# One product pair, the joining of product banks and four loads, rearranged in a decoder block on one core

## The chip, the cores and the metric

The kernel runs on one core of one Trainium2 chip. The metric is the device time of one execution in microseconds (us). Before the change, three runs took 1681.38, 1682.75 and 1682.48 us; the median is 1682.48 us. One further execution was profiled.

The core's engines work side by side and wait for each other by semaphores: TensorE (PE, matrix multiply; PEld is its weight load), VectorE (DVE), ScalarE (ACT), GpSimd (POOL) and SyncE (SP, which here only issues DMAs).

## The reference

One layer on 256 tokens of width 2048, in float32, cut to what matters:

```python
def token_mixers(x, ...):
    proj = x @ w_in                       # (256, 2048) x (2048, 13336)
    ...                                   # gated linear attention and forgetting attention
    merged = sigmoid(ma) * y_gla + sigmoid(mb) * y_fox
    return merged @ w_out

def conv_gated_mlp(x, w_gate, w_up, conv_w, conv_b, w_down):
    g = causal_dwconv(x @ w_gate, conv_w, conv_b)
    h = jax.nn.gelu(g) * (x @ w_up)       # (256, 5632)
    return h @ w_down

x = layer_norm(ALPHA * x + mix, ln1_g, ln1_b)
x = layer_norm(ALPHA * x + ffn, ln2_g, ln2_b)
x = x + sigmoid(x @ w_ple_gate) * (p @ w_ple_proj)
```

## The kernel before

**Split matmuls.** Every float32 operand is split in two: `hi`, a rounded copy made by ACT (`copy`, L106), and `lo = raw - hi`, made by DVE (L170). A product is three matmuls, hi by hi, hi by lo and lo by hi. Weights stream from memory in *units* of 1 MB (two tiles of 128 x 1024). `unit()` (L178) hands out the next unit and first calls `prep()` so that units up to two ahead are loaded and split: two DMAs on SP's queue into a ring of four `raw` tiles (L165, L166), then `hi` and `lo` into six buffers each. SP's instructions keep program order, set by hand (L108). On the other engines a planner orders the instructions before the run: it follows a clock of its own, takes what is ready there, higher priority first, and gives out buffers as it goes. The chip then executes each engine's list in that order.

**Half products.** `x_half` (L323) computes 256 tokens by 1024 columns: four PSUM banks (two token tiles t by two column blocks c), and a loop over units i, where a unit covers the pair of 128-row blocks 2i and 2i+1 of the contraction. A plain unit is 24 matmuls of 512 columns (`x_mm`, L267). After unit i it runs `mid[i]()` if there is one; that is where residual tiles and norm rows are loaded. Units kept for the *tail* are done bank by bank, so that banks finish one after the other, token tile 0 first; each is then evacuated by `evac`.

**Seven products.** Pairs listed in `ws` (`DNP`: pairs 2, 4, ..., 18 of each half of the down projection `dn`) are computed by `seven` (L283): the pair is a 2 x 2 block product, done with seven block products in place of eight, 21 matmuls. Three of them accumulate straight into the `dn` banks, four into product banks m0 to m3 (two from the pool of six `mm` banks, two from the pool of two `mx` banks) that live from the first such pair to the last. It needs sums of activation blocks, kept in DRAM (`hsd`, loaded by POOL's queue, L1095, L1096), and sums of weight blocks, made by `prep_seven` (L124: splits L135, four subtractions L140 to L143) and `split_seven` (L146: two further splits L153). A seven-product unit takes three buffers of 8 KB from the pool `big` (15 buffers): `raw` and two `ts`. hT, the MLP's activations, holds ten of them throughout `dn`; the two residual tiles `z2` and the norm rows come from the same pool.

**Joining.** After the last listed pair, `joined` (L928) adds the four product banks into the residual tiles: one ACT copy of m0 into `ju`, then eight DVE steps (L934 puts ALPHA z + sum into a tile, L938 adds a bank). Each tile z[t][:, block] then gets its own `dn` bank by `ev` (L919; L923, or L925 where there are no seven-product pairs) and its statistics (L926).

**Order of the stages.** Projections and attention; `wo` (two halves of eight units; residual tiles z1 and the first norm's gain and bias rows loaded after unit 4 of the first half, `mid1` at L998); first LayerNorm; gate and up projections; `dn` (two halves of 22 units; z2 loaded after unit 4 of the first half, `mid2` at L1157; norm rows after unit 8 of the second, `mid2a`, and the small operands of `pp` after unit 17, `mid2b`; tail of two units in the second half); second LayerNorm (`ln_out`, L827: statistics, normalisation L840 and L843, transposes on PE L846, scale and shift L853 and L855, split L857 and L858); the gate product `pg` (L1201) and the output. `pp` (24 matmuls, L988) is emitted after dn's last unit and depends on neither dn nor the LayerNorm. The residual evacuation and the statistics have the priority `P_STAT`; weight splits and the joining have none.

Of the kernel before, what the change touches and what calls it, by code (L numbers as in the profile page):

```python
# [14 lines left out]
ALU = mybir.AluOpType  # L15
# [8 lines left out]
NF = DFF // P  # L24
# [4 lines left out]
ALPHA = 2 ** 0.25  # L29
# [4 lines left out]
P_STAT = 5000  # L34
# [9 lines left out]
S8W = 2048  # L44
DN0 = 224
DNP = tuple(range(2, 20, 2))
WH = 1152
HSTEP = 48

# [5 lines left out]
def tile_block(ctx: ExitStack, tc: tile.TileContext, wu, wfv, wpp, xT_in, x_in, pT_in, wlr,  # L55
               chan, gnorm, lng, ident_in, mask_in, cmask_in, out):
    nc = tc.nc
# [15 lines left out]
    st1 = [cst.tile([P, 4, 6], F32, name=f"st1{t}") for t in range(2)]  # L73
# [13 lines left out]
    def w_tile(tag, dt, name, u):  # L87
        if tag == "lo":
            return wide.tile([P, 1024], dt, tag=tag, name=name)
        o = 0 if u in XSTAT else HSTEP  # L90
        return wide.tile([P, WH], dt, tag=tag, name=name)[:, o:o + 1024]

# [3 lines left out]
    def t2(name):  # L96
        return sm.tile([P, 512], F32, tag="t2", bufs=6, name=name)
# [7 lines left out]
    def copy(o, i, scale=1.0):  # L105
        nc.scalar.activation(o, i, AF.Copy, bias=0.0, scale=scale)  # L106
# [307 lines left out]
    for u in range(8):  # L414
        hi, lo = fvu[u]
        for j in range(2):
            kt = 2 * u + j
            a = xT[kt // 4][:, kt % 4, :]
            for cs in ((0,), (1,), (2,)) if u == 0 else ((0, 1, 2),):
                for t in range(2):  # L420
                    ah, al = a[:, t * P:t * P + P], a[:, 256 + t * P:256 + t * P + P]
                    for i, (w, x) in enumerate(((hi[j], ah), (lo[j], ah), (hi[j], al))):
                        for c in cs:
                            o, n = fch[c]
# [189 lines left out]
    for nm, dst, sc in (("q", gq, 1.0 / 16.0), ("k", gk, 1.0)):  # L614
        for n in range(8):
# [3 lines left out]
            h, c = n // 2, n % 2  # L619
# [178 lines left out]
    mT = [s8([P, 4, 512], F32R, name=f"mT{i}") for i in range(4)]  # L798
# [25 lines left out]
    x1d = dr.tile([2, P, 2048], F32, name="x1d")  # L824
# [84 lines left out]

        return stat, norm, turn  # L910

    def residual(name, act, K, zs, stats, mid, done=None, end=None, ws=()):

        for nh in range(2):
            def zp(t, c, nh=nh):
                g = 2 * nh + c
                return zs[t][:, g * 512:g * 512 + 512]

            def ev(t, c, ps, nh=nh, zp=zp):  # L919
                zc = zp(t, c)  # L920
                with tc.high_priority(P_STAT):
                    if ws:
                        nc.vector.tensor_tensor(zc, zc, ps, ALU.add)  # L923
                    else:
                        nc.vector.scalar_tensor_tensor(zc, zc, ALPHA, ps, ALU.mult, ALU.add)  # L925
                    nc.vector.bn_stats(stats[t][:, 2 * nh + c, :], zc)  # L926

            def joined(ms, zp=zp):  # L928
                p1, p5, p7, p6 = ms
                u = t2("ju")  # L930
                copy(u, p1)

                def onto(t, c, p):
                    nc.vector.scalar_tensor_tensor(zp(t, c), zp(t, c), ALPHA, p, ALU.mult,  # L934
                                                   ALU.add)

                def plus(o, a, p):
                    nc.vector.tensor_tensor(o, a, p, ALU.add)  # L938

                onto(0, 0, p1)  # L940
                plus(u, u, p6)
                onto(0, 1, u)
                plus(u, u, p7)
                onto(1, 0, u)
                plus(u, u, p5)
                onto(1, 1, u)
                plus(zp(0, 1), zp(0, 1), p5)

            x_half(f"{name}{nh}", act, K, ev, tail=2 if nh == 1 else 0, mid=mid[nh],
                   done=done if nh == 1 else None, end=end if nh == 1 else None, ws=ws,  # L950
                   joined=joined)

    def affine(zs, gb_, after, gs=range(4)):
# [15 lines left out]
    def ple_prep(half):  # L969

        w = [s8([P, 2048], F32R, name=f"pw{half}{i}") for i in range(2)]
        pt_ = s8([P, 2, 512], F32R, name=f"pTs{half}")
        pTs = [pt_[:, k, :] for k in range(2)]
        for k in range(2):
            raw = ring.tile([P, 1024], F32, tag="raw", bufs=4, name=f"praw{half}{k}")
            nc.sync.dma_start(raw, wpp[half, :, k * 1024:k * 1024 + 1024])
            o = slice(k * 1024, k * 1024 + 1024)
            copy(w[0][:, o], raw)
            nc.vector.tensor_tensor(w[1][:, o], raw, w[0][:, o].bitcast(F32), ALU.subtract)
        pT = t2("pTr").rearrange("p (k t) -> p k t", t=S)  # L980
        nc.sync.dma_start(pT, pT_in)
        for k in range(2):
            copy(pTs[k][:, 0:256], pT[:, k, :])
            nc.vector.tensor_tensor(pTs[k][:, 256:512], pT[:, k, :],
                                    pTs[k][:, 0:256].bitcast(F32), ALU.subtract)
        return w, pTs
# [8 lines left out]
    z1 = [s8([P, 2048], name=f"z1{t}") for t in range(2)]  # L995
    gain = [None, None]

    def mid1():  # L998
        for t in range(2):
            nc.sync.dma_start(z1[t], x_in[t])  # L1000
        gain[0] = load_gain(0)

    x1T = [s8([P, 4, 512], F32R, name=f"x1T{g}") for g in range(4)]
    pq, first = [], []
# [68 lines left out]
                    turn1(G[3])  # L1073
            first.extend(ps)

    residual("wo", mT, 16, z1, st1, ({4: mid1}, {3: lambda: pq.append(ple_prep(0))}), end=end1)
    mixers.append(affine(z1, gain[0], lambda t: nc.gpsimd.dma_start(x1d[t], z1[t]),
                         [g for g in range(4) if g not in AFF_DVE]))

# [7 lines left out]
    hT = [None] * 11  # L1087
    hsd = dr.tile([len(DNP), P, 2, 512], F32, name="hsd")
    before = [None]

    def h_sums(i):
        j = DNP.index(i)

# [4 lines left out]
        return load  # L1098

    for nh in range(2):  # L1100
        for i in DNP:
            sums[DN0 + nh * (NF // 2) + i] = h_sums(i)

    def lt(shape, dt, name):
# [10 lines left out]
    for n in range(NF):  # L1115
# [17 lines left out]
        u = t1("up")  # L1133
# [4 lines left out]
        nc.vector.tensor_tensor(dst[:, 256:512], y, dst[:, 0:256].bitcast(F32), ALU.subtract)  # L1138
        if n % 2 == 1 and n // 2 in DNP:
            sf = t2("hs")  # L1140
            x_sums(before[0], y, sf)
            for i, nm in enumerate(("hsh", "hsl")):
# [4 lines left out]
                else:  # L1147
                    nc.vector.tensor_tensor(sp, sf, sh.bitcast(F32), ALU.subtract)
                nc.gpsimd.dma_start(hsd[DNP.index(n // 2), :, i, :], sp.bitcast(F32))
        before[0] = y  # L1150
# [3 lines left out]
    z2 = [s8([P, 2048], name=f"z2{t}") for t in range(2)]  # L1154
    st2 = [st20, sm.tile([P, 4, 6], F32, tag="st2", bufs=1, name="st21")]

    def mid2():  # L1157
        for t in range(2):
            nc.sync.dma_start(z2[t], x1d[t])

    def mid2a():
        gain[1] = load_gain(1)
# [5 lines left out]
    pb, pq = [], []  # L1168
# [3 lines left out]
            pb.extend(ple_proj(1, *pq[0]))  # L1172
        ln_out(z2, st2, t, x2T, c_g2, c_b2, "l2", P_LN2[t])

    residual("dn", hT, NF, z2, st2, ({4: mid2}, {8: mid2a, NF // 2 - 5: mid2b}), done2, ws=DNP)
    pp = [s8([P, 2, 1024], name=f"ppk{i}") for i in range(2)]
    for t in range(2):
        for c in range(2):
# [37 lines left out]
def _xst(w):  # L1216

    k, n = w.shape
    a = w.reshape(k // 256, 2, P, n // 1024, 1024).transpose(3, 0, 2, 1, 4)
    return a.reshape((k // 256) * (n // 1024), P, 2048)  # L1220


def _swap(a, ps):

    a = a.reshape(-1, P, 4, 512)
    for n in ps:
        a[n] = a[n][:, [0, 1, 3, 2]]
    return a.reshape(-1, P, 2048)
# [7 lines left out]
def _chan(v):  # L1236
    return v.reshape(-1, P).T


def _layout(i):  # L1240
    w_in = i["w_in"][0]
    c = lambda nm, n: w_in[:, OFF[nm]:OFF[nm] + n]
    bg, bf = _wst(i["w_branch_gla"][0]), _wst(i["w_branch_fox"][0])
    br = []
    for n in range(16):
        br.append(bg[n:n + 1])
        if n % 2 == 0:
            br.append(bf[n // 2:n // 2 + 1])
    gu = np.stack([_wst(i["w_gate"][0]), _wst(i["w_up"][0])], 1).reshape(2 * NF, P, 2048)
    wu = np.concatenate(  # L1250
        [_wst(c("fq", 1024)), _wst(c("fk", 1024)), _wst(c("gq", 1024)),
         _wst(c("gk", 1024)), _xst(c("gv", 2048)), _xst(c("gr", 2048)),
         _wst(c("ma", 2048)), _wst(c("mb", 2048))] + br
        + [_xst(i["w_out"][0]), gu, _swap(_xst(i["w_down"][0]), [h * (NF // 2) + p for h in range(2) for p in DNP]),
           _xst(i["w_ple_gate"][0])], 0)
    wfv = np.concatenate([c("fv", 1024), c("glr", 16), c("ff", 8)], 1)
    wfv = wfv.reshape(8, 2, P, NS).transpose(0, 2, 1, 3)
    x = _fold(i["x"][0])
    bfo = np.zeros((P, 1), np.float32)
    bfo[:FH, 0] = i["b_forget"][0]  # L1260
    chan = np.concatenate(
        [_chan(i["b_gla_lr"][0]), bfo, _chan(i["ln1_g"][0]), _chan(i["ln1_b"][0]),
         _chan(i["ln2_g"][0]), _chan(i["ln2_b"][0])]
        + [_chan(i["conv_w"][0][j]) for j in range(3)] + [_chan(i["conv_b"][0])], 1)
    lng = np.stack([i["ln1_g"], i["ln1_b"], i["ln2_g"], i["ln2_b"]])
    s = np.arange(P)[:, None]
    t = np.arange(P)[None, :]
    masks = [s == t]
    for lev in range(1, 8):
        L = 1 << lev  # L1270
        masks.append((s // L == t // L) & (s % L < L // 2) & (t % L >= L // 2))
    mask = np.stack([m if h == 0 else m.T for m in masks for h in range(2)], 1).astype(np.float32)
    caus = np.where(t <= s, 0.0, NEG).astype(np.float32)
    cmask = np.concatenate([caus.T, caus], 1)
    return dict(wu=wu, wfv=wfv, wpp=_xst(i["w_ple_proj"][0]), xT=x.T.reshape(16, P, S).transpose(1, 0, 2),
                x=x.reshape(2, P, D), pT=_fold(i["p"][0, 0]).T.reshape(2, P, S).transpose(1, 0, 2),
                wlr=i["w_gla_lr"][0], chan=chan, gnorm=i["gla_norm_g"], lng=lng,
                ident=np.eye(P, dtype=np.float32), mask=mask, cmask=cmask)
# [20 lines left out]
```

## Time and profile before

| | |
|---|---|
| Profiled execution, time | 1681.58 us |
| Its span (first to last instruction) | 1679.8 us |
| Median of three runs | 1682.48 us |
| Mean granted TensorE clock | 0.996 |
| Busy: DVE, ACT, POOL | 71%, 52%, 4% |
| Moved by DMA | 344.39 MB, mean 205 GB/s |
| Matmul records | 8981 |

How to read it: busy time is the union of an engine's instructions, as a share of the span. Matmuls overlap in the pipeline and their ends are modelled, so PE can look busy while it issues fewer matmuls than it could; the count of matmuls in a window tells more. In a line of an engine's order the number in square brackets is the engine's idle time before the instruction, with what ended it. In a line of the waits stand total, times and longest. Times in windows and orders count from the span's start. `L170` is line 170 of the kernel. A few matmul records can be missing from a trace.

### The profile page before, as it was taken

Reading aid. Unit: us, or ns where it says so; the run is one execution under the profiler, and the core shown is the slowest. Engines: PE = TensorE matmul, PEld = TensorE weight load, DVE = VectorE, ACT = ScalarE, POOL = GpSimd, SP = SyncE. Lnnn points to the kernel's source line nnn. Section 1 sums busy time; section 2 is a strip of 40 time slices with the busy share of each in tenths; the row PEclk is TensorE's granted clock in tenths of the full one; section 3 lists DMA queues with packets and bytes.
Section 4 is the critical chain, followed back from the end, with each engine's and each line's share of the span. In section 5 each row is a group of like instructions: output and inputs, shape, how many; then the busy total and the mean of one; then the engine's idle time right before and its main releaser. Section 6 shows DMA issues by size and latency. Waiting matters only on the chain.

```text
span 1679.8 us, 24075 instructions
## 1 busy us (share of the span) xinstructions
PE 1659.1 (99%) x8981; PEld 1435.6 (85%) x8981; DVE 1196.8 (71%) x1757; ACT 866.5 (52%) x1247; POOL 64.5 (4%) x177
## 2 busy tenths in 40 slices
PE   9999999999999999999999999999999999999898
PEld 8888888888888888888788888888888887788687
DVE  6666658768756557774677777777777778998774
ACT  5645445545555544443465555555555545455543
POOL 0100000000000000000010000000000011010000
PEclk9999999999999999999999999999999999999999
DMA  7755455555555455557646676666666666696455
GB/s 268 266 191 164 163 189 182 180 177 176 184 179 175 165 195 192 195 192 258 236 152 209 229 232 206 205 207 205 209 204 208 216 248 222 236 338 245 150 180 171
DMA packets 95748, 344.39 MB, mean 205 GB/s; under 512 B 11096, under 2 KB 12768, under 8 KB 94224
## 3 DMA queue, kind: packets, MB, share of 16 engines
q1 hardware_dynamic: 90528, 324.51, 57.7%
q0 software_dynamic: 5104, 18.36, 2.9%
q8 instruction: 70, 1.15, 0.3%
q14 instruction: 46, 0.38, 0.1%
HBM read 332.85 MB, written 9.97 MB: 204 GB/s over the span
## 4 chain that ended last, share of the span: by engine, by line
PE 94%; DVE 2%; DMA 1%; ACT 1%; issue 1%; SPq 0%; POOL 0%; ACTq 0%; DVEq 0%
PE psu L236 9%; PE psg L236 9%; PE dn L280 7%; PE psm L236 7%; PE gr L280 5%; PE gv L280 5%; PE pg L280 5%; PE psu L238 5%; PE psg L238 5%; PE wo L280 4%; PE psm L238 3%; PE psa L236 3%; PE fv L425 2%; PE dn L301 2%; PE psfq L236 2%; PE psfk L236 2%
## 5 line engine op out<-in xcount | busy, mean ns | idle before, releaser
L106 ACT ACTIVATE hi<-raw 128x1024 fp32r<-128x1024 f32 (+1 forms) x568 | 591.7, 1045 | 635.4 <-issue 220.8
L170 DVE TENSOR_TENSOR lo<-raw,hi 128x1024 fp32r<-128x1024 f32 x532 | 649.4, 1222 | 359.8 <-ACT hi L106 356.8
L236 PE MATMUL psu<-x1T,hi 128*128 128x512 f32 x688 | 236.0, 389 | 0.0
L236 PE MATMUL psg<-x1T,hi 128*128 128x512 f32 x672 | 230.5, 389 | 0.0
L238 PE MATMUL psu<-x1T,lo 128*128 128x256 f32 x688 | 190.0, 276 | 0.0
L238 PE MATMUL psg<-x1T,lo 128*128 128x256 f32 x672 | 185.5, 276 | 0.0
L236 PE MATMUL psm<-xT,hi 128*128 128x512 f32 x512 | 175.8, 391 | 0.0
L236 PEld LDWEIGHTS psu<-x1T,hi 128*128 128x128 f32 x688 | 129.1, 188 | 26.8
L236 PEld LDWEIGHTS psg<-x1T,hi 128*128 128x128 f32 x672 | 126.2, 188 | 26.3
L238 PE MATMUL psm<-xT,lo 128*128 128x256 f32 x512 | 141.5, 276 | 0.0
L238 PEld LDWEIGHTS psu<-x1T,lo 128*128 128x128 f32 x688 | 129.2, 188 | 0.0
L238 PEld LDWEIGHTS psg<-x1T,lo 128*128 128x128 f32 x672 | 126.1, 188 | 0.0
L280 PE MATMUL dn<-hi,hT 128*128 128x512 f32 x416 | 118.9, 389 | 0.0
L236 PEld LDWEIGHTS psm<-xT,hi 128*128 128x128 f32 x512 | 96.2, 188 | 19.8
L238 PEld LDWEIGHTS psm<-xT,lo 128*128 128x128 f32 x512 | 96.2, 188 | 0.1
L280 PEld LDWEIGHTS dn<-hi,hT 128*128 128x128 f32 x416 | 78.0, 188 | 16.3
L236 PE MATMUL psa<-oT,hi 128*128 128x512 f32 x256 | 87.8, 389 | 0.0
L280 PE MATMUL wo<-hi,mT 128*128 128x512 f32 x256 | 71.9, 396 | 3.1 <-DVE z L925 3.0
L280 PE MATMUL gv<-hi,xT 128*128 128x512 f32 x256 | 72.3, 394 | 0.0
L280 PE MATMUL gr<-hi,xT 128*128 128x512 f32 x256 | 72.1, 394 | 0.0
L238 PE MATMUL psa<-oT,lo 128*128 128x256 f32 x256 | 70.7, 276 | 0.0
L280 PE MATMUL pg<-hi,x2T 128*128 128x512 f32 (+1 forms) x256 | 69.7, 383 | 0.0
(300 smaller groups left out, 2836.4 us busy)
## 6 DMA issues: line engine op xcount, KB each, us to landing
raw<-in_wu_dram SPq DMA_DIRECT2D x568, 512.0 KB, 4.6
fvraw<-in_wfv_dram SPq DMA_DIRECT2D x14, 524.0 KB, 7.9
hi<-hsd POOLq DMA_DIRECT2D x18, 256.0 KB, 4.8
lo<-hsd POOLq DMA_DIRECT2D x18, 256.0 KB, 5.4
lnb<-in_lng_dram SPq DMA_DIRECT2D x4, 1024.0 KB, 11.7
hsd<-hsh POOLq DMA_DIRECT2D x9, 256.0 KB, 5.6
hsd<-hsl POOLq DMA_DIRECT2D x9, 256.0 KB, 5.4
z<-in_x_dram SPq DMA_DIRECT2D x2, 1024.0 KB, 10.8
```

The costliest lines, as they stand in the source:

```text
L106: nc.scalar.activation(o, i, AF.Copy, bias=0.0, scale=scale)
L170: nc.vector.tensor_tensor(lo, raw, hi.bitcast(F32), ALU.subtract)
L236: nc.tensor.matmul(ps, lhsT=hi[i // 8 if hoff == 0 else 0][:, w0 % 1024:w0 % 1024 + P], rhs=a[:, kt % 4, :], start=first and i == 0, stop= ...
L238: nc.tensor.matmul(ps[:, 256:512], lhsT=lo[i // 8 if hoff == 0 else 0][:, w0 % 1024:w0 % 1024 + P], rhs=a[:, kt % 4, 0:256], start=False, ...
L280: nc.tensor.matmul(bs[j][:, 0:m], lhsT=x, rhs=v[:, o:o + m], start=first and i == 0, stop=last and i == 2)
L301: nc.tensor.matmul(ps, lhsT=a, rhs=v, start=m and first and i == 0, stop=m and last and i == 2)
L425: nc.tensor.matmul(fbk[t][c][:, 0:n], lhsT=x, rhs=w[:, o:o + n], start=kt == 0 and i == 0, stop=kt == 15 and i == 2)
```

## The change

Four things. In the second half of `dn` the last seven-product pair (18) becomes a plain pair, so the joining there follows pair 16. The joining's copy and its eight DVE steps get the priority `P_STAT` in both halves. The two z1 tiles are loaded after units 2 and 3 of `wo`'s first half and the norm rows after unit 5, in place of all four after unit 4. The two z2 tiles are loaded after units 3 and 7 of dn's first half, in place of both after unit 4.

```diff
+DNW = (DNP, DNP[:-1])
...
-    def residual(name, act, K, zs, stats, mid, done=None, end=None, ws=()):
+    def residual(name, act, K, zs, stats, mid, done=None, end=None, ws=((), ())):
...
-                    if ws:
+                    if ws[nh]:
                         nc.vector.tensor_tensor(zc, zc, ps, ALU.add)
...
                 p1, p5, p7, p6 = ms
                 u = t2("ju")
-                copy(u, p1)
 
                 def onto(t, c, p):
-                    nc.vector.scalar_tensor_tensor(zp(t, c), zp(t, c), ALPHA, p, ALU.mult,
-                                                   ALU.add)
+                    with tc.high_priority(P_STAT):
+                        nc.vector.scalar_tensor_tensor(zp(t, c), zp(t, c), ALPHA, p, ALU.mult,
+                                                       ALU.add)
 
                 def plus(o, a, p):
-                    nc.vector.tensor_tensor(o, a, p, ALU.add)
+                    with tc.high_priority(P_STAT):
+                        nc.vector.tensor_tensor(o, a, p, ALU.add)
+
+                with tc.high_priority(P_STAT):
+                    copy(u, p1)
 
                 onto(0, 0, p1)
...
-                   done=done if nh == 1 else None, end=end if nh == 1 else None, ws=ws,
+                   done=done if nh == 1 else None, end=end if nh == 1 else None, ws=ws[nh],
...
-    def mid1():
-        for t in range(2):
-            nc.sync.dma_start(z1[t], x_in[t])
+    def mid1(t):
+        nc.sync.dma_start(z1[t], x_in[t])
+
+    def mid1g():
         gain[0] = load_gain(0)
...
-    residual("wo", mT, 16, z1, st1, ({4: mid1}, {3: lambda: pq.append(ple_prep(0))}), end=end1)
+    residual("wo", mT, 16, z1, st1, ({2: lambda: mid1(0), 3: lambda: mid1(1), 5: mid1g}, {3: lambda: pq.append(ple_prep(0))}), end=end1)
...
-        for i in DNP:
+        for i in DNW[nh]:
             sums[DN0 + nh * (NF // 2) + i] = h_sums(i)
...
-    def mid2():
-        for t in range(2):
-            nc.sync.dma_start(z2[t], x1d[t])
+    def mid2(t):
+        nc.sync.dma_start(z2[t], x1d[t])
...
-    residual("dn", hT, NF, z2, st2, ({4: mid2}, {8: mid2a, NF // 2 - 5: mid2b}), done2, ws=DNP)
+    residual("dn", hT, NF, z2, st2, ({3: lambda: mid2(0), 7: lambda: mid2(1)}, {8: mid2a, NF // 2 - 5: mid2b}), done2, ws=DNW)
...
-        + [_xst(i["w_out"][0]), gu, _swap(_xst(i["w_down"][0]), [h * (NF // 2) + p for h in range(2) for p in DNP]),
+        + [_xst(i["w_out"][0]), gu, _swap(_xst(i["w_down"][0]), [h * (NF // 2) + p for h in range(2) for p in DNW[h]]),
```

## The prediction

> **What bounds the kernel now.** I read the page first, then the waits of TensorE (PE), the busy times in windows of 20 us, and the order of instructions of single engines where those windows fall short.
>
> ```profile
> PE 1659.1 (99%) x8981; PEld 1435.6 (85%) x8981; DVE 1196.8 (71%) x1757; ACT 866.5 (52%) x1247; POOL 64.5 (4%) x177
> ```
>
> PE is the bound. A faster kernel needs fewer matmuls or less lost PE time. Lost time is more than the idle time, since a matmul's modelled end covers small gaps, so I count matmuls. Windows: bounds, length, then PE, PEld, DVE, ACT, POOL busy (count), granted clock, DMA share, GB/s.
>
> ```profile
> 780.00:800.00 20.00, 20.00 (x90) 16.57 (x89) 7.31 (x6) 6.37 (x6) 0.00 (x0) 1.00 0.75 272
> ...
> 800.00:820.00 20.00, 16.90 (x67) 13.29 (x66) 12.78 (x15) 8.29 (x8) 0.00 (x0) 0.91 0.59 198
> ...
> 1380.00:1400.00 20.00, 19.38 (x84) 15.43 (x83) 11.61 (x14) 7.41 (x8) 2.13 (x4) 1.00 0.65 228
> 1400.00:1420.00 20.00, 19.91 (x86) 15.46 (x85) 16.43 (x18) 10.46 (x11) 1.06 (x2) 1.00 0.61 220
> 1420.00:1440.00 20.00, 19.20 (x82) 14.56 (x81) 17.00 (x20) 12.24 (x15) 1.06 (x2) 1.00 0.68 244
> ...
> 1560.00:1580.00 20.00, 15.78 (x73) 12.68 (x71) 16.21 (x28) 7.69 (x9) 2.05 (x2) 0.99 0.48 160
> 1580.00:1600.00 20.00, 17.82 (x81) 14.94 (x82) 13.99 (x27) 17.91 (x36) 0.00 (x0) 0.83 0.23 75
> ```
>
> A full window of 512-column matmuls holds 90. The pace comes from the chain of waits, from the end's transposes in the groups by line, and from PE's order of instructions:
>
> ```profile
> 1443.67 22.90 PE dn L280 x101
> ```
> ```profile
> L846 PE MATMUL ptl<-ident,z 128*128 128x128 f32 x32 | 5.5, 312 | 6.4 <-DVE z L840 3.7 <-ACT lny L853 2.7
> ```
> ```profile
> 1569.76 4.92 PE L280 MATMUL pp<-pw,pTs 128*128 128x512 f32 x21
> 1578.38 1.09 PE L846 MATMUL ptl<-ident,z 128*128 128x128 f32 x8 [3.70 <-DVE z L840]
> ...
> 1583.80 1.20 PE L280 MATMUL pg<-hi,x2T 128*128 128x512 f32 x2
> ```
>
> A matmul takes 22.90 / 101 = 0.227 us. Three places near the change lose time: 800 to 820 (the seam between the halves of wo) 23 matmuls, 5.2 us; 1380 to 1440 (first half of dn) 6 + 4 + 8 = 18, 4.1 us; 1560 to 1600 (end of dn, second LayerNorm) 40 us less 122 matmuls (27.7) and 32 transposes at 1.09 / 8 (4.4), 7.9 us. Together 17.2 us, which is the most that the change can win.
>
> **Part 1: the loads of z1 and the norm rows (wo).** SP's order, then DVE's, then two short windows:
>
> ```profile
> 769.32 0.90 SPq L1000 DMA_DIRECT2D z<-in_x_dram  x2
> 770.27 2.42 SPq L966 DMA_DIRECT2D lnb<-in_lng_dram  x2
> 772.79 30.43 SPq L166 DMA_DIRECT2D raw<-in_wu_dram  x11
> ```
> ```profile
> 789.67 4.87 DVE L170 TENSOR_TENSOR lo<-raw,hi 128x1024 fp32r<-128x1024 f32 x4 [9.92 <-ACT hi L106]
> ...
> 801.64 1.23 DVE L170 TENSOR_TENSOR lo<-raw,hi 128x1024 fp32r<-128x1024 f32 x1 [1.65 <-ACT hi L106]
> 802.78 2.47 DVE L925 SCALAR_TENSOR_TENSOR z<-z,wo 128x512 f32<-128x512 f32 x4
> ```
> ```profile
> 780.00:782.00 2.00, 2.00 (x11) 1.65 (x10) 0.00 (x0) 0.00 (x0) 0.00 (x0) 1.00 1.01 422
> ...
> 806.00:808.00 2.00, 2.00 (x6) 1.54 (x6) 2.00 (x4) 1.02 (x1) 0.00 (x0) 0.50 0.13 51
> ```
>
> Four loads of 1 MB sit ahead of the weights; at 422 GB/s they hold the queue for 10 us, and DVE stands idle 9.92 us. The splits never catch up before wo's first half ends: the first evacuation (z, L925) waits behind a split at 801.64 and starts at 802.78. PE idles for its banks, then runs at clock 0.50. After the change the loads go out one, one and two at a time, over three units. A unit is 24 matmuls, 5.4 us, and brings 1 MB (193 GB/s), so each unit's time has room for one more MB. One z1 tile adds 2.5 us of queue, the rows together 5. The 9.92 us wait left PE whole (90 in 780 to 800), so the weights run at least 10 us ahead: arrears of 5 are worked off before 800, where 10 were not. The same four DMAs are issued, all on SP's queue; z1 is wanted only at 800, the rows later. Gain 0 (the wait moves to the rows) to 5.2; I take 4.8, nearer the full size, because half of the arrears come two units earlier.
>
> Of the 5.2 us, 3.1 are idle (20 less 16.90) and the other 2.1 follow from clock 0.50. The Trainium skill (TensorE: Matmul & The Clock Gate, Part 1) says that it takes an idle window of about 3.4 us to halve the clock. Here 3.1 was enough, and the measurement decides. By the rule a wait of 3 us left over would cost 3, by this row 5.
>
> **Part 2: z2's two loads (first half of dn).** SP's order, seven-product loads at L129 and residual loads at L1159:
>
> ```profile
> 1353.96 3.82 SPq L1159 DMA_DIRECT2D z<-x1d  x2
> ...
> 1366.52 0.81 SPq L129 DMA_DIRECT2D raw<-in_wu_dram  x2
> ...
> 1380.66 0.81 SPq L129 DMA_DIRECT2D raw<-in_wu_dram  x2
> ...
> 1393.36 0.80 SPq L129 DMA_DIRECT2D raw<-in_wu_dram  x2
> ...
> 1404.75 0.80 SPq L129 DMA_DIRECT2D raw<-in_wu_dram  x2
> ...
> 1415.58 0.80 SPq L129 DMA_DIRECT2D raw<-in_wu_dram  x2
> ```
>
> Two units need 24 + 21 matmuls, 10.2 us. The seven-product loads come 14.1, 12.7, 11.4 and 10.8 us apart: they, not PE, set the pace. Each pair takes three 8 KB buffers (raw and two ts) from the pool, where hT holds ten of fifteen, and the z2 tiles take the other two from 1354 on. So a load waits for the pair before it. With the second z2 tile behind pair 9 instead of pair 6, one buffer stays with the weights until about 1370, and the load of 1366.52 or of 1380.66 no longer waits. What that hides is a landing, once:
>
> ```profile
> raw<-in_wu_dram SPq DMA_DIRECT2D x568, 512.0 KB, 4.6
> ```
>
> A lead of 4.6 us would cover the 4.1 lost; but the loop stays at 10.8 against 10.2 afterwards, and the first z2 now goes ahead of pair 6's load (2.5 us of queue). Bounds: a loss of 2.0 (z2 delays that load and no buffer is won) and a gain of 4.1. I take 2.0, 4.6 less 2.5.
>
> **Part 3: join early, pair 18 plain (end of dn).** DVE's order, then its groups between 1338 and 1580:
>
> ```profile
> 1549.51 0.69 DVE L934 SCALAR_TENSOR_TENSOR z<-z,dn1m 128x512 f32<-128x512 f32 x1 [1.94 <-ACT ju L106]
> ...
> 1565.20 0.69 DVE L923 TENSOR_TENSOR z<-z,dn 128x512 f32<-128x512 f32 x1 [1.89 <-PE dn L280]
> ...
> 1569.87 0.68 DVE L938 TENSOR_TENSOR z<-z,dn1m 128x512 f32<-128x512 f32 x1
> 1570.46 1.28 DVE L923 TENSOR_TENSOR z<-z,dn 128x512 f32<-128x512 f32 x2
> ...
> 1572.85 1.21 DVE L170 TENSOR_TENSOR lo<-raw,hi 128x1024 fp32r<-128x1024 f32 x1
> ```
> ```profile
> L170 DVE TENSOR_TENSOR lo<-raw,hi 128x1024 fp32r<-128x1024 f32 x53 | 64.2, 1217 | 4.7 <-ACT hi L106 4.7
> L153 DVE TENSOR_TENSOR ts<-raw,ts 128x1024 fp32r<-128x1024 f32 x36 | 44.0, 1223 | 4.3 <-ACT ts L106 3.3
> ...
> L141 DVE TENSOR_TENSOR raw<-raw 128x512 f32<-128x512 f32 x18 | 12.5, 692 | 1.3 <-DMA raw<-in_wu_dram 0.8
> ```
>
> The join spreads over 20 us, from 1549.51 to 1570.55, behind splits. Its last sum (1569.87) goes into the tile of bank (0,1), which the first token tile's LayerNorm needs; by the loop, 24 matmuls of the second token tile follow that bank, and dn ends at 1569.8, so it is done by 1564.3; the first evacuation was released by PE at 1565.20, so I say 1565.5. So the evacuation is 5 us late (1570.46). From there to the first gate matmul (1583.80) it is 13.3 us, with splits between the steps (1572.85).
>
> After: pair 16 is the last joined, 10 us earlier; eight DVE steps of 0.69 are done by about 1552, behind nothing that the end needs. Pair 18 plain costs 3 matmuls, 0.7 us. It takes from DVE a split of 512 and one of 1024, four subtractions and two ts splits (0.69 + 1.22 + 4 x 0.69 + 2 x 1.22 = 7.1) and adds two splits (2.4): 4.7 us less; four ACT copies become two; two 256 KB loads on POOL's queue go. All that lies beside PE.
>
> The chain starts at 1565.5 + 0.7, and up to 9 pp matmuls (2.0 us) may be drawn ahead of it, because their banks come free early: 1566.2 to 1568.2. At the old 13.3 us the gates start by 1581.5: 2.3 earlier. With three splits fewer between the steps, 9.6 us, they start by 1577; PE's own work (pp until 1574.7, 0.7, sixteen transposes at 2.2) ends at 1577.6 in any case, 6.2 earlier, and with waits under 3 us the slow clock (0.83 in 1580 to 1600) goes too. Bounds: 0 (the chain takes up new splits) and 7.2 (7.9 less 0.7). I take 5.2 net, nearer the upper, because DVE has 4.7 us less to do just before.
>
> In the first half the join moves ahead of splits too. PE loses nothing there now (101 matmuls in one piece from 1443.67); the splits wait 8 x 0.69 = 5.5 us longer with about one unit (5.4) in hand: nothing, or up to 2, within part 2's bounds.
>
> **Sum.** 4.8 + 2.0 + 5.2 = 12.0. The profiled execution took 1681.58 (span 1679.8 and 1.8 around it): 1669.6. The median of the runs before is 0.9 above the profiled one: 1670.5. All best bounds give 16.5 less, 1666.0; wo at 4.8 with dn at its worst (-2, 0) 1679.7.
>
> **The rivals.**
>
> *The end stays as it is.* The planner draws pp ahead and puts new splits into the gaps of the LayerNorm chain, which then begins earlier but ends where it did. For it: splits already stand there (1572.85), and pp is the only cover after dn. Against: DVE has 4.7 us less to do. Then 4.8 + 2.0 less 0.7: 1676.4.
>
> *It does not do what it says.* Priority only counts for what is ready in the planner's own clock, so the join may keep its place; the rows' 2 MB may hold wo's splits just as the four did. For it: L923 has the same priority and still stood behind. Against: it stood behind the join itself, and the arrears halve. About 1682.
>
> *Slower.* DVE and ACT work through one order. A join set early stands at the head and waits for the seventh product, with the splits of the next units behind it; already now L934 waited 1.94 us there. If that wait is W, PE stands for what W and 5.5 us of join exceed one unit (5.4). At W = 8 (most of a 10.8 us pair) each half loses 8.1 and 2.1 for the clock: 20.4, less 4.8 + 2.0 + 3 elsewhere: 10.6 more, 1693. It decides from W = 3 on, where 2 x (3.1 + 2.1) exceeds the 9.8 won. Against: between 1549.51 and 1565.20 splits and join alternate with room. The Trainium skill (TensorE: Matmul & The Clock Gate, Architectural detail) states that ACT and DVE queues are strict FIFO, which speaks against moving a waiting step forward; the trace agrees, as L925 at 802.78 did not pass the split at 801.64.
>
> **How the numbers follow.** Forecast 0.62 (its own range 1666 to 1675); end unchanged 0.17; no effect 0.11; slower 0.10. Leaving out most of the last, and a little on the low side for a PE that loses less than the counts show, the range is 1664.5 to 1681. A change of 0.2%, 3.4 us, is what this measurement tells from none: faster 0.62 + 0.17 + 0.03 = 0.82, within 0.08, slower 0.10.
>
> **What would show it.** Part 1: 800 to 820 holds 90 matmuls at clock 1.00, and DVE's 9.92 us wait is gone. Part 2: seven-product loads under 12.7 us apart, and fewer than 18 matmuls short. Part 3: L934 and L938 of the second half in one run before 1556; L923 within 1 us of PE's bank; the gates before 1579. It is wrong if PE idles in the units after a join, or if the transposes still wait over 3 us.

## The result, and the profile after

The changed kernel took 1671.38 us (median of four runs, 1668.56 to 1672.02), the kernel before on the same chip 1681.93 (four runs, 1679.61 to 1682.75). The ratio is 0.9936, 95% interval 0.9919 to 0.9953: 10.5 us or 0.64% faster. The profiled execution took 1670.91 us, with a span of 1669.1. The forecast was 1670.5.

First the page's engine line of the changed kernel. PE has three matmuls more (pair 18) and yet 2.1 us less busy time (1657.0 against 1659.1). Fewer of its matmuls run at the slow clock: the windows below have a granted clock of 0.91 twice before the change and 1.00 throughout after it.

```profile
PE 1657.0 (99%) x8984; PEld 1432.4 (86%) x8984; DVE 1191.5 (71%) x1751; ACT 864.6 (52%) x1245; POOL 65.4 (4%) x175
```

Then four windows of the kernel before and the same four after: the seam of wo, dn's first half from 1360 to 1440 (80 us, so that small shifts in time matter little), the units after the join in dn's second half (called the second join here), and the end. The number in brackets behind PE's busy time counts its matmuls, and it is what to compare:

```profile
800.00:820.00 20.00, 16.90 (x67) 13.29 (x66) 12.78 (x15) 8.29 (x8) 0.00 (x0) 0.91 0.59 198
1360.00:1440.00 80.00, 78.49 (x338) 62.02 (x337) 61.05 (x67) 40.78 (x44) 6.38 (x12) 1.00 0.68 244
1540.00:1560.00 20.00, 20.00 (x90) 16.55 (x89) 15.99 (x19) 11.14 (x13) 0.00 (x0) 1.00 0.52 170
1560.00:1600.00 40.00, 33.59 (x154) 27.62 (x153) 30.19 (x54) 25.60 (x44) 2.05 (x2) 0.91 0.36 117
```
```profile
800.00:820.00 20.00, 20.00 (x90) 16.57 (x89) 14.13 (x16) 9.66 (x11) 0.00 (x0) 1.00 0.68 218
1360.00:1440.00 80.00, 78.74 (x339) 62.10 (x338) 65.39 (x73) 41.32 (x45) 6.38 (x12) 1.00 0.68 244
1540.00:1560.00 20.00, 19.10 (x81) 14.73 (x80) 16.97 (x21) 10.08 (x11) 0.00 (x0) 1.00 0.78 264
1560.00:1600.00 40.00, 40.00 (x193) 32.82 (x192) 35.72 (x60) 29.02 (x47) 1.11 (x2) 1.00 0.58 192
```

The seam is full (90 against 67) and the end is full (193 against 154, at clock 1.00). In these two profiles the first half of dn is as it was (339 against 338), and one window has become worse: 1540 to 1560 holds 81, where 90 stood.

**The seam.** DVE's order after the change (the number in square brackets is the idle time before the row). The wait of 9.92 us has shrunk to 3.67, and the first evacuation (L926, L925 before) comes at 799.02 with no split running late before it:

```profile
789.18 2.42 DVE L171 TENSOR_TENSOR lo<-raw,hi 128x1024 fp32r<-128x1024 f32 x2 [3.67 <-ACT hi L107]
...
799.02 2.47 DVE L926 SCALAR_TENSOR_TENSOR z<-z,wo 128x512 f32<-128x512 f32 x4
```

**dn's first half.** SP's order after the change; the z2 loads stand at L1164, the seven-product loads at L130 (dots stand for rows left out):

```profile
1347.69 0.33 SPq L1164 DMA_DIRECT2D z<-x1d  x1
1349.05 0.80 SPq L130 DMA_DIRECT2D raw<-in_wu_dram  x2
...
1359.20 0.80 SPq L130 DMA_DIRECT2D raw<-in_wu_dram  x2
...
1369.40 0.33 SPq L1164 DMA_DIRECT2D z<-x1d  x1
1375.45 0.81 SPq L130 DMA_DIRECT2D raw<-in_wu_dram  x2
...
1388.44 0.80 SPq L130 DMA_DIRECT2D raw<-in_wu_dram  x2
```

One load gets its buffer at PE's own pace (1349.05 to 1359.20, 10.2 us). Then the second z2 tile goes first, and the next two loads come 16.2 and 13.0 us apart. What was won once is handed back.

**The join and the end.** ACT's and DVE's order at the second join, and below it DVE's evacuations (L924) and PE's order at the end:

```profile
1534.00 0.60 ACT L107 ACTIVATE ju<-dn1m 128x512 f32<-128x512 f32 x1 [8.08 <-PE dn1m L302]
```
```profile
1534.63 0.69 DVE L935 SCALAR_TENSOR_TENSOR z<-z,dn1m 128x512 f32<-128x512 f32 x1 [7.45 <-ACT ju L107]
1535.23 0.69 DVE L143 TENSOR_TENSOR raw<-raw 128x512 f32<-128x512 f32 x1
...
1551.64 0.69 DVE L935 SCALAR_TENSOR_TENSOR z<-z,ju 128x512 f32<-128x512 f32 x1
...
1559.36 0.69 DVE L924 TENSOR_TENSOR z<-z,dn 128x512 f32<-128x512 f32 x1 [0.82 <-PE dn L281]
```
```profile
1557.46 0.50 PE L281 MATMUL dn<-lo,hT 128*128 128x512 f32 x1 [0.76 <-DVE lo L171]
...
1566.72 1.09 PE L847 MATMUL ptl<-ident,z 128*128 128x128 f32 x8
...
1568.12 2.70 PE L281 MATMUL pp<-pw,pTs 128*128 128x512 f32 x11
...
1574.53 0.39 PE L281 MATMUL pg<-hi,x2T 128*128 128x512 f32 x1
```

The join's last step is over at 1552.33, seven us before the first evacuation, which now waits for PE and for nothing else. The first eight transposes fit in before dn's last matmuls, pp covers the next eight, and the gates start at 1574.53 where they started at 1583.80. But ACT stood idle 8.08 us before the join's copy and DVE 7.45 us before its first sum, and some 20 us later PE waits for a split (0.76 us, and small gaps around it): those are the nine matmuls missing in 1540 to 1560. The join in dn's first half waited for nothing (its copy starts at 1429.30 with no idle time before it), and 1440 to 1460 holds 90 before and after.

### The profile page after: what moved, and what is told of

Same layout as the page of the kernel before. It is cut to its first block, busy times and chain, and to the rows that moved or that the text cites. A ratio compares the mean times of both kernels' runs of the same rounds, so it can differ in the third digit from the quotient of the medians.

```text
span 1669.1 us, 24069 instructions
## 1 busy us (share of the span) xinstructions
PE 1657.0 (99%) x8984; PEld 1432.4 (86%) x8984; DVE 1191.5 (71%) x1751; ACT 864.6 (52%) x1245; POOL 65.4 (4%) x175
## 4 chain that ended last, share of the span: by engine, by line
PE 94%; DVE 2%; DMA 2%; ACT 1%; issue 1%; SPq 0%; POOL 0%; ACTq 0%; DVEq 0%
PE psu L237 9%; PE psg L237 9%; PE psm L237 7%; PE dn L281 6%; PE gr L281 5%; PE gv L281 5%; PE wo L281 5%; PE pg L281 5%; PE psu L239 5%; PE psg L239 5%; PE psm L239 4%; PE psa L237 3%; PE fv L426 2%; PE psfq L237 2%; PE psfk L237 2%; PE psq L237 2%
## 5 line engine op out<-in xcount | busy, mean ns | idle before, releaser
L237 PEld LDWEIGHTS psu<-x1T,hi 128*128 128x128 f32 x688 | 129.2, 188 | 26.7
L239 PEld LDWEIGHTS psu<-x1T,lo 128*128 128x128 f32 x688 | 129.2, 188 | 0.0
L281 PE MATMUL dn<-hi,hT 128*128 128x512 f32 x432 | 124.3, 390 | 0.1
L281 PE MATMUL dn<-lo,hT 128*128 128x512 f32 x216 | 70.5, 393 | 1.2 <-DVE lo L171 1.2
```

The lines of the kernel that those rows point to most:

```text
L237: nc.tensor.matmul(ps, lhsT=hi[i // 8 if hoff == 0 else 0][:, w0 % 1024:w0 % 1024 + P], rhs=a[:, kt % 4, :], start=first and i == 0, stop= ...
L239: nc.tensor.matmul(ps[:, 256:512], lhsT=lo[i // 8 if hoff == 0 else 0][:, w0 % 1024:w0 % 1024 + P], rhs=a[:, kt % 4, 0:256], start=False, ...
L281: nc.tensor.matmul(bs[j][:, 0:m], lhsT=x, rhs=v[:, o:o + m], start=first and i == 0, stop=last and i == 2)
```

## The experiments

Eleven more runs followed, on two chips: nine edited kernels, and the kernel before and the changed kernel once more. Each was compared with runs of the kernel before that were interleaved on its own chip (median 1679.64 to 1680.34 us there). Only ratios are compared between runs that were not interleaved with each other. The table gathers them. "before" and "changed" mark the kernel that was edited; the last four columns count PE's matmuls in windows of its profile like those above.

| kernel | median us | ratio to before, 95% | 800-820 | 1360-1440 | 1540-1560 | 1560-1600 |
|---|---|---|---|---|---|---|
| before, shown above | 1681.93 | | 67 | 338 | 90 | 154 |
| before, again (one execution) | 1678.38 | | 90 | 323 | 90 | 154 |
| before + wo loads apart | 1679.63 | 0.9993 [0.9982, 1.0005] | 90 | 323 | 90 | 153 |
| before + z2 loads apart | 1677.92 | 0.9990 [0.9979, 1.0001] | 85 | 339 | 90 | 155 |
| before + both load edits | 1676.87 | 0.9982 [0.9972, 0.9993] | 90 | 339 | 90 | 153 |
| before + priority alone | 1678.85 | 0.9995 [0.9984, 1.0005] | 74 | 331 | 90 | 169 |
| before + pair 18 plain alone | 1673.32 | 0.9965 [0.9952, 0.9978] | 87 | 317 | 90 | 192 |
| changed, shown above | 1671.38 | 0.9936 [0.9919, 0.9953] | 90 | 339 | 81 | 193 |
| changed, again | 1672.09 | 0.9962 [0.9948, 0.9976] | 90 | 338 | 84 | 191 |
| changed, old wo loads | 1673.19 | 0.9961 [0.9947, 0.9974] | 88 | 336 | 84 | 190 |
| changed, no priority | 1671.18 | 0.9950 [0.9935, 0.9964] | 90 | 340 | 90 | 192 |
| changed, z2 late | 1669.07 | 0.9934 [0.9920, 0.9947] | 90 | 349 | 86 | 190 |
| changed, z2 late, no priority | 1666.60 | 0.9929 [0.9916, 0.9942] | 90 | 347 | 90 | 188 |

**The parts of the change, one at a time.** The wo loads alone, on the kernel before:

```diff
-    residual("wo", mT, 16, z1, st1, ({4: mid1}, ...
+    residual("wo", mT, 16, z1, st1, ({2: lambda: mid1(0), 3: lambda: mid1(1), 5: mid1g}, ...
```

> The kernel before with one part of the change: z1 and the norm rows of wo loaded apart. Theory (the 4 MB in front of the weights made the seam's wait, and the clock fell after it): 5.2 us less than before, about 1676.7; 90 matmuls in the 20 us around the seam; nothing else moves. Rival (the rows alone still hold the splits, and what the changed kernel won at the seam needs another part): 0 to 2 us less.

1679.63 us against 1680.34, ratio 0.9993 [0.9982, 1.0005]: not told from nothing, although the profile has a whole seam. The 5.2 us of the theory did not come. The windows say where that went:

```profile
800.00:820.00 20.00, 20.00 (x90) 16.53 (x90) 14.26 (x17) 9.91 (x11) 0.00 (x0) 1.00 0.67 209
1360.00:1440.00 80.00, 76.74 (x323) 60.35 (x322) 59.11 (x65) 39.34 (x42) 6.38 (x12) 0.98 0.63 222
```

The 23 matmuls of the seam are there, and 15 of those that dn's first half had are gone. That asked for a second profile of the kernel before.

Pair 18 plain alone, with neither the priority nor the loads:

```diff
+DNW = (DNP, DNP[:-1])
...
-                   done=done if nh == 1 else None, end=end if nh == 1 else None, ws=ws,
+                   done=done if nh == 1 else None, end=end if nh == 1 else None, ws=ws[nh],
```

> The kernel before with one part of the change: pair 18 of the second half plain, the joining with no priority, all loads as before. Theory (what brings the join forward at the end is that it follows pair 16, two units sooner, not its priority): 5 to 7 us less than before, 1675 to 1677; the transposes wait for nothing over 1 us. Rival (the priority does it; without it the join spreads behind splits as before): at most 2 us less.

1673.32 us against 1680.34, 7.0 us less, ratio 0.9965 [0.9952, 0.9978]. PE's order at its end:

```profile
1569.69 0.39 PE L281 MATMUL dn<-hi,hT 128*128 128x512 f32 x1
1569.91 1.98 PE L281 MATMUL pp<-pw,pTs 128*128 128x512 f32 x8
1571.73 1.03 PE L847 MATMUL ptl<-ident,z 128*128 128x128 f32 x8
...
1577.38 0.62 PE L281 MATMUL pg<-hi,x2T 128*128 128x512 f32 x2
```

Its dn ends where that of the kernel before did (pp at 1569.91 against 1569.76), so the two can be laid on each other: 7.5 us from there to the gates in place of 14.0. PE's own work in between is 24 matmuls of pp at 0.227 and sixteen transposes of 2.2 together, 7.6: nothing is lost any more. The plain pair alone gives the whole gain of the end (192 matmuls in 1560 to 1600, 193 in the changed kernel). It does two things at once, and no run separates them: the join follows pair 16, and DVE has less to do just before the end.

The priority alone (pair 18 stays with seven products, the old loads):

```diff
-                copy(u, p1)
+                with tc.high_priority(P_STAT):
+                    copy(u, p1)
...
+                    with tc.high_priority(P_STAT):
                         nc.vector.scalar_tensor_tensor(zp(t, c), zp(t, c), ALPHA, p, ...
```

> The kernel before with one part of the change: priority for the joining's copy and eight steps, pair 18 still a seven-product pair, all loads as before. Theory (priority moves only the copy and the first step, and these wait for PE at the head of ACT's and DVE's queues): within 2 us of before, rather slower, and ACT idle over 3 us before the copy in the second half. Rival (priority brings the join before the end): 4 us less or more than that.

1678.85 against 1680.34, ratio 0.9995 [0.9984, 1.0005]: nothing that can be told. DVE's order shows what the priority moved and what it did not:

```profile
1549.63 0.69 DVE L935 SCALAR_TENSOR_TENSOR z<-z,dn1m 128x512 f32<-128x512 f32 x1 [4.71 <-ACT ju L107]
...
1563.02 0.68 DVE L935 SCALAR_TENSOR_TENSOR z<-z,ju 128x512 f32<-128x512 f32 x1
```

The first sum now stands ahead of a split and waits 4.71 us (1.94 before) for a bank that PE has not finished; it starts no earlier than it did (1549.51 before). The steps behind it are what came earlier: the last is over at 1563.70, 6.9 us sooner than before (1570.55), still with splits between them. ACT's wait before the copy is 2.56 us, as before, and not the over 3 that was expected. Its profile has 15 matmuls more in 1560 to 1600 than before, 3.4 us; the runs show 1.5 us less, with an interval from 2.7 less to 0.8 more. So a gain at the end is not shown by the times, and not excluded either.

The changed kernel without the priority (the three `with` lines of the joining taken out):

> The changed kernel without the priority of the joining. Theory (the 8 us that ACT waits for the first product bank make splits and loads late, and cost the about 2 us that PE loses at 1556): 1 to 2.5 us less than the changed kernel, about 1669.5; no ACT wait over 4 us before the copy and no short window between 1520 and 1560. Rival (the priority is worth something at the end): 2 us or more above the changed kernel.

1671.18 us, ratio 0.9950 [0.9935, 0.9964], between those of the changed kernel's two comparisons (0.9936 and 0.9962): neither the 1 to 2.5 us of the theory nor the rival can be told. 1540 to 1560 holds 90 again, as the theory said, but ACT still waits 6.69 us before the copy, against it.

**How steady is the kernel before?** The kernel before once more, for a second profile:

> The kernel before, unchanged, for a second profile. The single profile of before shows 5.2 us lost at the seam of wo and about 4 in 1380 to 1440; the runs of the first experiments lost 0 to 5 at the seam (where the loads of wo were old) and 5 to 8 in dn's first half. Theory (both losses depend on how late a landing is, and vary from run to run): one of the two differs by over 1.5 us from the first profile. Rival (they are fixed by the order of the lists): both within 0.5 us of it.

1678.38 us. The windows, and DVE's order at the seam:

```profile
800.00:820.00 20.00, 20.00 (x90) 16.57 (x89) 14.48 (x16) 10.00 (x11) 0.00 (x0) 1.00 0.64 214
1360.00:1440.00 80.00, 76.61 (x323) 60.04 (x322) 59.51 (x65) 38.57 (x41) 6.26 (x12) 0.98 0.63 223
```
```profile
784.51 1.22 DVE L170 TENSOR_TENSOR lo<-raw,hi 128x1024 fp32r<-128x1024 f32 x1 [7.18 <-ACT hi L106]
...
797.15 2.47 DVE L925 SCALAR_TENSOR_TENSOR z<-z,wo 128x512 f32<-128x512 f32 x4
```

These are the same instructions in the same order, yet the four loads kept DVE waiting for 7.18 us and not 9.92, the first evacuation came at 797.15 and not 802.78, and the seam lost nothing. Instead dn's first half lost 15 matmuls more. So the 23 matmuls on which the first term of the prediction rests were one execution's. Over the six profiles with the old wo loads the seam held 67, 90, 85, 87, 74 and 88; with the new loads it held 90 in all seven.

The z2 loads alone, on the kernel before:

```diff
-    residual("dn", hT, NF, z2, st2, ({4: mid2}, ...
+    residual("dn", hT, NF, z2, st2, ({3: lambda: mid2(0), 7: lambda: mid2(1)}, ...
```

> The kernel before with one part of the change: z2's tiles loaded after units 3 and 7 of dn's first half. Theory (pair 8's load goes out 2 us sooner, ahead of POOL's loads of sums, and the collision that cost dn's first half 1 to 5 us in the profiles with the old loads is gone): 1380 to 1440 loses 3 to 4 us in place of 4 to 8, the median falls by 1 to 4 us. Rival (the extra buffer is given back by z2 in front of pair 6's load, and nothing changes): within 1 us of before.

1677.92 us against 1679.64, ratio 0.9990 [0.9979, 1.0001]: 1.7 us less, within what was expected, and not quite told from nothing.

The changed kernel with the old wo loads:

> The changed kernel with the loads of z1 and the norm rows put back after unit 4 in one piece. Theory (the seam's loss returns, at its usual 0.5 to 5 us): 2 to 4 us above the changed kernel, 1673.5 to 1675.5. Rival (what the seam loses, dn's first half no longer loses, as the sums of both in the profiles suggest, 9.0, 7.2, 8.9 and 10.0 us): within 1 us of the changed kernel.

1673.19 us, ratio 0.9961 [0.9947, 0.9974]. The seam lost 2 matmuls.

The changed kernel again, beside the next two:

> The changed kernel, unchanged, beside the others on one chip and for a second profile. Theory (its losses at the seam and in dn's first half no longer depend on a late landing): seam 0, 1380 to 1440 3 to 4 us lost as in its first profile, median 8 to 10 us below before, ratio 0.994 to 0.9955. Rival (its first profile was a lucky one): seam or first half lose over 1.5 us more.

1672.09 us against 1680.27, ratio 0.9962 [0.9948, 0.9976]; it is 8.2 us less, and its interval overlaps that of the first comparison, barely. The losses in the profile are as in the first one, as expected (seam full, 338 matmuls in dn's first half). Beside it the kernel with the old wo loads (0.9961) is no slower.

Both load edits together, on the kernel before:

> The kernel before with both load edits (wo and z2), pair 18 a seven-product pair and no priority. Theory (each load edit alone is masked by the other loss, as the first half of dn loses more where the seam loses less): 4 to 6 us less than before, more than the 0.0007 and 0.0010 of the two alone together. Rival (the effects add as measured): 2 to 3 us less.

1676.87 us against 1680.27, 3.4 less, ratio 0.9982 [0.9972, 0.9993]. The loads together are worth something, about half of what the forecast gave them. The result lies between the two sums expected (4 to 6 us, and 2 to 3).

The table shows why one load edit hides in the other. Add the counts of the first two windows. With the old z2 loads they make 405, 413, 413, 405 and 404, whatever the wo loads are: what the seam saves, dn's first half loses. With z2 apart they make 424 (old wo loads, twice) and 428, 429, 429 and 430 (new ones). So in the profiles the wo edit shows its worth only once z2 is mended, and it is 5 matmuls, 1.1 us. The times cannot tell so little: 0.9990 against 0.9982 on the kernel before, 0.9961 against 0.9962 on the changed one.

The windows stand at fixed times, while dn begins at times up to 7 us apart. Measured from each stage's own first matmul, the grouping is the same. The time of wo (first to last matmul) and of dn's first half (its first matmul to the first of the second half) add up to 208.5 to 211.4 us in the five profiles with the old z2 loads, 205.8 and 205.9 with z2 apart and the old wo loads, and 204.5 to 204.9 with both apart.

**Is it the buffer?** The theory for dn's first half was that a z2 tile takes a buffer of the seven-product pairs. If so, loading z2 later than the seven-product pairs' busiest stretch should bring the loads to PE's pace. The changed kernel with:

```diff
-({3: lambda: mid2(0), 7: lambda: mid2(1)}, ...
+({12: lambda: mid2(0), 15: lambda: mid2(1)}, ...
```

> The changed kernel with z2's tiles loaded after units 12 and 15 of dn's first half, so that both buffers serve the weights until then. Theory (three buffers make the loop of 10.5 to 10.8 us against PE's 10.2, and what 1380 to 1440 still loses): under 5 matmuls short there, 2.5 to 3.5 us less than the changed kernel, about 1668. Rival (the loop is DVE's own work of 9.5 us and a landing, and buffers do not matter): within 1 us of the changed kernel.

1669.07 us, ratio 0.9934 [0.9920, 0.9947]. SP's order:

```profile
1347.17 0.80 SPq L130 DMA_DIRECT2D raw<-in_wu_dram  x2
...
1357.32 0.80 SPq L130 DMA_DIRECT2D raw<-in_wu_dram  x2
...
1367.52 0.80 SPq L130 DMA_DIRECT2D raw<-in_wu_dram  x2
...
1377.72 0.80 SPq L130 DMA_DIRECT2D raw<-in_wu_dram  x2
...
1387.92 1.30 SPq L130 DMA_DIRECT2D raw<-in_wu_dram  x2
1389.39 0.33 SPq L1164 DMA_DIRECT2D z<-x1d  x1
...
1399.48 0.80 SPq L130 DMA_DIRECT2D raw<-in_wu_dram  x2
...
1409.68 0.33 SPq L1164 DMA_DIRECT2D z<-x1d  x1
1414.26 0.80 SPq L130 DMA_DIRECT2D raw<-in_wu_dram  x2
```

The seven-product loads come 10.2 us apart, two units of PE, until the z2 tiles are there; then they come 11.6 and 14.8 apart. dn's first half holds 349 matmuls, 10 more than in the changed kernel, and the whole 80 us at 0.227 would be 353. (1380 to 1440 is 6 short of 270, where under 5 was expected.) wo and dn's first half together take 202.6 us, 2 less than with both loads apart. A z2 load also holds the queue, so the buffer is not the only thing that moved; but what the seven-product loads waited for speaks for it. Between 1340 and 1440 SP's waits are, in the kernel before and with z2 late:

```profile
SPq L129 <- DVE ts L153: 51.2, 7, 8.3
```
```profile
SPq L130 <- PE dn0m L302: 41.3, 5, 8.5
```

The numbers are total, times and longest. Before, the loads waited mostly for DVE to split a pair ahead of them; with z2 late they wait mostly for PE to use one, and only 6.0 us for DVE. (The profile infers what released a wait.)

**The best of all.** z2 late and no priority:

> The changed kernel without the priority of the joining and with z2's tiles loaded after units 12 and 15. Theory (the priority only makes ACT wait for the product bank; late z2 gives the first half of dn its buffers): as the run with late z2 or up to 2 us less, ratio 0.992 to 0.9935, no loss over 0.5 us in 1540 to 1560. Rival (the priority is worth something once dn's first half is mended): 1 us or more above the run with late z2, ratio over 0.994.

1666.60 us (1664.96 to 1668.74), ratio 0.9929 [0.9916, 0.9942], on a chip where the changed kernel took 1672.09 (1669.24 to 1672.57): no run of the one is as long as the shortest of the other. It beats both kernels. This is what the theory said (0.992 to 0.9935, nothing lost in 1540 to 1560); from the run with late z2 alone (0.9934) it cannot be told. ACT's and DVE's order at its second join, to lay beside the changed kernel's:

```profile
1532.23 0.60 ACT L107 ACTIVATE ju<-dn1m 128x512 f32<-128x512 f32 x1 [7.18 <-PE dn1m L302]
```
```profile
1525.28 0.68 DVE L143 TENSOR_TENSOR raw<-raw 128x512 f32<-128x512 f32 x1
...
1533.81 2.36 DVE L171 TENSOR_TENSOR lo<-raw,hi 128x1024 fp32r<-128x1024 f32 x2 [6.11 <-ACT hi L107]
...
1538.36 0.68 DVE L934 SCALAR_TENSOR_TENSOR z<-z,dn1m 128x512 f32<-128x512 f32 x1
...
1548.30 0.69 DVE L934 SCALAR_TENSOR_TENSOR z<-z,ju 128x512 f32<-128x512 f32 x1
```

The copy waits 7.18 us on ACT without any priority, so most of the 8.08 belongs to the plain pair (with pair 18 a seven-product pair it is 2.56). That the planner fills less work in ahead of the join is a likely reason, not one that was tried. What the priority adds is the order on DVE. Here a subtraction of pair 16 (L143) runs at 1525.28, seven us ahead of the copy, and the first split after the wait comes before the first sum; with the priority the sum goes first, and L143 and the split stand behind it until 1535.23 and later. All four profiles with pair 18 plain and the priority fall short in 1540 to 1560 (81, 84, 84, 86), the three without it do not (90 each): a price of 4 to 9 matmuls, 0.9 to 2.0 us. From the first matmul of dn's second half to the first gate matmul the four take 123.6 to 125.1 us, the three 121.9 to 123.1. In the times alone the price is within the intervals. By the same measure the kernels with pair 18 a seven-product pair take 128.3 to 129.2 us, and 125.5 with the priority alone: there it is worth about 3 us in its one profile, and with the plain pair nothing is left for it to win. That the late subtraction and split are what PE meets 20 us later is read from the order; it was not tried by itself.

## Why the prediction was right, point by point

**The bound and the places.** PE was the bound, and in the first pair of profiles the time came out of two of the three places named. That the total, 10.5 us against 12.0, came so close is in part luck: the loads were sized too large (6.8, measured 3.4) and the plain pair too small (5.2, measured 7.0).

**Part 1, wo: right mechanism, term too large.** The row that was to show it did: 90 matmuls at clock 1.00, first evacuation at 799.02. DVE's wait shrank to 3.67, it is not gone. The term of 4.8 was taken from one profile in which the seam lost 23 matmuls. It measured 0.7 alone, not told from nothing; beside the new z2 loads the profiles put it at 1.1, which the times cannot tell. The step that failed is the last one, in which the whole loss of one execution was made a gain of the median. Another execution of the same kernel lost nothing there. (Of the 5.2 the prediction put 2.1 down to the slow clock; the windows at 0.74, 0.50 and 0.91 from 804 to 810 make that 1.7.) The rival that the wait moves elsewhere (the lower bound, 0) was nearer than the value taken, though it moved not to the norm rows but to dn's first half.

**Part 2, z2: the size held, by another way.** The prediction traded one hidden landing (4.6) for a longer queue (2.5) and left the loop at 10.8 us. As measured, the edit alone gave 1.7 (interval from no gain to 3.5), close to the 2.0. But the check named for it failed: the loads were to come under 12.7 us apart, and two came 16.2 and 13.0 apart; the other, fewer than 18 matmuls short in 1380 to 1440, was met by little (16). The buffer argument itself was right, and late z2 shows that it was worth more: with no z2 tile in the pool the loop does not stay at 10.8, it runs at 10.2. That the second tile would take the buffer again at pair 9, before its lead was used, is what the step left out.

**Part 3, the plain pair: right, term too small.** The term was 5.2 with an upper bound of 7.2; the plain pair alone gave 7.0. The prediction saw that PE's own work would end in time, and then kept a discount for splits between the steps. In the run there was no such loss: 7.5 us from dn's end to the gates against 7.6 of PE's work. The join ended at 1552.33, forecast "by about 1552"; the transposes no longer wait.

**Part 3, the join ahead of splits: wrong.** It was to put the eight steps in one run before 1556, behind nothing. They were done by then, but spread over 17.7 us (1534.63 to 1552.33) among splits; without the priority they took 10.6 (1538.36 to 1548.99 in the best kernel). With the plain pair, then, the priority set the first sum ahead of splits, where it had to wait, and the last step hardly gained by it (over 15.6 us before dn's last matmul begins, 14.1 without the priority). With pair 18 a seven-product pair it did bring the last step 6.9 us forward, but again not in one run. A likely reason, read from the orders and not tried: a step that waits for the step before it is not ready in the planner's clock when the next split is, and then a priority has nothing to choose from. That is the rival "it does not do what it says", true in part and of this part alone. That the end still came out right is due to the plain pair, which gives all of it without the priority.

**The rival "slower".** Its mechanism is in the trace of the second half: W is 8.08 on ACT and 7.45 on DVE, beyond the 3 us from which it was to decide, and PE idles in the units after the join, which was named as a sign of being wrong. Its price was not there: 1540 to 1560 lost 9 matmuls, 2.0 us, where the sum gave 8.1 and 2.1 for the clock in each half. In the first half W was nothing and PE lost nothing, as part 3 had said. The sum took one unit of work in hand when the join began to wait. PE went on for some 20 us before the wait at 1557.46, so more was split by then, and only a small part of the 8 us reached PE. The strict FIFO of the Trainium skill (TensorE: Matmul & The Clock Gate, Architectural detail) agrees with this trace: L143 ran behind L935 at 1535.23, after the whole wait. A queue that stands is not yet a PE that stands.

**The sum.** Loads 3.4 (forecast 6.8) and plain pair 7.0 (forecast 5.2) make 10.4; the whole change measured 10.5 in the first comparison and 8.2 in the second. The 1 to 2 us that the priority costs in the profiles would account for a part of the difference, and the intervals are as wide as the rest.

**What stays open.** Why the same loads take longer in one execution than in another, and why dn's first half makes up for a whole seam when z2 is loaded the old way, so that the sum of both windows stays between 404 and 413. The times at which dn begins differ by a few us with the seam's loss, and the loads of dn then meet those of POOL's queue at other moments; whether that is the reason was not tried. Open too is how much of the plain pair's 7.0 us comes from the earlier join and how much from the work that DVE is spared.

## What to carry to other kernels

Before a stall is priced from one profile, look at a second profile of the same kernel: a loss that depends on when loads land can move to another stage, while a loss that follows from a fixed order was the same in both profiles here (the late join: 154 matmuls at the end in each). A residual tile that shares a pool with the weights should be loaded as late as its use allows, since here a buffer lent early slowed the loads behind it. And to bring a chain of dependent steps forward, move what it waits for, as the plain pair did. A priority can set a step ahead of work that is ready, and on an engine that works in order that step then holds up what stands behind it.

## What was not expected of the hardware

The clock fell after shorter waits than the prediction reckoned with (it said that with waits under 3 us the slow clock goes too). In the second profile of the kernel before, PE's order and its windows of 2 us show a wait of 2.00 us, after a last matmul that began at 1385.97:

```profile
1388.37 0.50 PE L301 MATMUL dn0m<-ts,hi 128*128 128x512 f32 x1 [2.00 <-ACT ts L106]
```
```profile
1386.00:1388.00 2.00, 0.36 (x2) 0.00 (x0) 2.00 (x3) 0.74 (x1) 0.00 (x0) 1.00 0.18 47
1388.00:1390.00 2.00, 1.26 (x3) 0.67 (x4) 1.50 (x2) 0.31 (x1) 0.00 (x0) 0.70 0.99 307
1390.00:1392.00 2.00, 2.00 (x6) 1.52 (x6) 0.99 (x2) 1.01 (x2) 0.00 (x0) 0.50 0.97 358
1392.00:1394.00 2.00, 2.00 (x10) 1.65 (x9) 1.97 (x3) 1.46 (x2) 0.00 (x0) 0.95 0.84 328
```

The granted clock was at 0.50 within 4 us and nearly back in the window from 1392. The three windows at 0.70, 0.50 and 0.95 lack 0.6, 1.0 and 0.1 us of full clock: the 2.4 us without a new matmul cost 1.7 us more in slow ones. The Trainium skill (TensorE: Matmul & The Clock Gate, Part 1) gives an idle window of about 3.4 us; the measured waits here are 3.0 and 2.00, and the measurement decides.

The other surprise is told above: two executions of one kernel, with the same instructions in the same order, lost 23 matmuls at the seam or none, and their times differ by no more than the runs do (1681.58 and 1678.38 us).
